# Macaron decoder layer on one core: order of the Strassen products, of the weight loads and of the norm statistics changed

## The chip, the core and the metric

The kernel runs on one core of a Trainium2 chip. The metric is device time in microseconds (us) of one execution of the whole layer; lower is better. TensorE is written PE, VectorE DVE, ScalarE ACT, GpSimd POOL, and SyncE SP, which issues most of the DMAs.

## The reference

One layer on x of 1024 tokens by 1024 features, float32, D_FF = 2816 (22 tiles of 128). The parts that the change touches are the two SwiGLU feed-forward networks (FFN) and the norms around them:

```python
h = rms_norm(x, ffn1_norm); x = x + 0.5 * (silu(h @ w_gate) * (h @ w_up)) @ w_down
h = rms_norm(x, mix_norm);  z = h @ w_in + b_in
...
x = x + merged @ w_out
h = rms_norm(x, ffn2_norm); x = x + 0.5 * (silu(h @ w_gate) * (h @ w_up)) @ w_down
return rms_norm(x, final_norm)
```

Between the FFNs stands a mixer: sliding-window attention and an mLSTM in parallel, gated and merged.

## The kernel before

All tensors lie with features on the 128 partitions and tokens along the free axis; the tokens are two halves of HS = 512, and x is KT = 8 feature tiles. TensorE multiplies with numbers split in two (`parted`, L325 to L328: ACT writes the high part, L327, VectorE the low part, L328), so every float32 product is three matmuls, high by high, high by low, low by high.

**Each FFN is done with seven products in place of eight** (a Strassen-Winograd scheme over the two halves of the tokens and two halves of the contracted features and of the columns). `PRODUCTS` (L29) gives the order of the products: 1, 2, 6, 7, 4, 5, 3. `gate_up` (L371) runs over 11 sets of a gate tile and an up tile, and in each set over the seven products, each in two groups w = 0 (gate) and 1 (up) of 12 matmuls at L413. `order` inside it lists (set, product): the first products 1 and 2 of the first LEAD = 4 sets come first, since they need only the first half of the tokens, then product 6 to 3 set by set. A weight block of 128x1024 is loaded by `load`, combined by `sum_of` (L403), and split one product ahead by `split`, into four rotating buffers `whi` and `wlo`. The products accumulate in PSUM banks `mm` (8, rotating); `product` (L404) lets product 2 write on into the bank of product 1 and product 3 into that of product 5:

```python
            key = {2: 1, 3: 5}.get(p, p)
            if first:
                st["ps", s, key, w] = psum.tile([128, HS], F32, name="mm")
```

so the first matmul of product 2 waits for ACT's copy of product 1 (L452), and that of product 3 for VectorE's sum with product 5 (L461). `gated` makes the SwiGLU (tanh on ACT, L421; two VectorE operations, L424 and L425). After a set, `paired` splits its results and stores them to `gd` in DRAM.

**The down part** (`ffn`) has 21 steps: three chunks (DOWN: 4, 4 and 3 column tiles) of seven products, each of 48 matmuls (L626; 36 in the last chunk). The moving operand of a step is fetched one step ahead from `gd` on POOL's queue (`fetch`, L564, 2 MB, two buffers); the weight blocks `dn` of a chunk, four of 1 MB (0.75 MB in the last), come on SP's queue (`load`, L555): for chunk 0 at the end of the last set's product 2, for chunk 1 at the end of its product 5, for chunk 2 at the step (1, 1). Results are added to x (L668, L669), and in the last chunk `done1` or `done2` adds up the squares of each finished x (`stats`: ACT square L252, VectorE add L254).

**The norms.** `rstd_of` (L256) sums the squares over the partitions by small matmuls (L261), adds epsilon (L263) and raises to -1/2 on POOL (L264); two turns later it spreads the result over the partitions by four transposes (L269, copy L271). `mixed` (L330) scales the second half of the tokens (L341) and makes the combined operands of products 6, 7, 4, 5, 3. `norm` (L282) scales the first half for the mixer: VectorE L297, ACT L298 for the high part, POOL L300 for the low part. These are generators: `lead` is advanced by `gate_up` between groups, those in `bg` by `pump`, one turn each; a `yield` is a turn, and so the number of turns sets where the work stands in each engine's queue. Engines run their instructions in program order.

**The order of the whole**: FFN 1, norm, mixer for the first 512 tokens, its residual at L1398, norm of the second half, mixer for the second half, its residual at L1469 (with `early` scaling the first half for FFN 2, L1437), FFN 2, final norm (`final`, L1497 and L1499).

## Time and profile before

| | |
|---|---|
| time, three executions | 2474.77, 2476.14 (median), 2485.99 us |
| the profiled execution | 2482.01 us, span 2479.4 us |
| TensorE busy | 2365.1 us, 95% |
| VectorE busy | 1740.1 us, 70% |
| ScalarE busy | 944.0 us, 38% |
| GpSimd busy | 258.0 us, 10% |
| mean granted TensorE clock | 0.976 of full |
| DMA | 361.44 MB, mean 146 GB/s |

The span is the time from the first to the last instruction in the profile. A busy time is a sum over an engine's instructions; the rows below place them. A timeline row gives start and duration (both in us), engine, line and operation, then tiles written and read, the count, and in brackets the idle time just before it and what ended that. The granted clock (PEclk) is 1.00 at the level of 2.4 GHz and 0.50 at 1.2 GHz.

### The profile page before, as it was taken

What the parts mean: (1) busy time and instruction counts of PE and PEld (TensorE: products, weight loads), DVE (VectorE), ACT (ScalarE), POOL (GpSimd) and SP (SyncE); (2) the same over time, 40 slices, a digit from 0 to 9 for tenths busy, and PEclk for the clock granted to TensorE, in tenths of its full rate; (3) what the DMA queues carried; (4) which work ended last, traced back from release to release, by engine and by line L of the source; (5) the groups of instructions that cost most, each with busy time, mean ns of one, the idle gap of its engine ahead of it and who ended that gap; (6) DMA issues with size and microseconds to landing.
All of it is one profiled execution on the core that took longest, in us unless ns stands there. A gap on an engine that the chain in (4) does not pass through costs nothing.

```text
span 2479.4 us, 30117 instructions
## 1 busy us (share of the span) xinstructions
PE 2365.1 (95%) x11094; PEld 1956.3 (79%) x11094; DVE 1740.1 (70%) x2780; ACT 944.0 (38%) x1664; POOL 258.0 (10%) x246
## 2 busy tenths in 40 slices
PE   7899999999998999999999999999899999999996
PEld 6788888778777878888877778888677888887885
DVE  6898888765768864554658944545589987886666
ACT  4333343312236642333346632333343443332223
POOL 0000000000044320000233400000000000000001
PEclk8999999999999999999999999999899999999997
DMA  4354453995631223222532122223524544569754
GB/s 172 100 197 163 153 165 132 339 319 187 208 126 52 73 62 92 75 81 84 173 109 64 52 79 87 79 79 99 186 98 162 191 148 146 171 231 331 250 176 138
DMA packets 154324, 361.44 MB, mean 146 GB/s; under 512 B 13505, under 2 KB 22849, under 8 KB 154177
## 3 DMA queue, kind: packets, MB, share of 16 engines
q1 hardware_dynamic: 131728, 277.79, 34.3%
q0 software_dynamic: 21584, 81.53, 9.6%
q8 instruction: 87, 1.43, 0.2%
q14 instruction: 61, 0.49, 0.1%
q10 hardware_dynamic: 864, 0.21, 0.0%
HBM read 263.27 MB, written 96.21 MB: 145 GB/s over the span
## 4 chain that ended last, share of the span: by engine, by line
PE 51%; DVE 12%; DMA 3%; ACT 3%; issue 3%; SPq 0%; DVEq 0%; POOL 0%; ACTq 0%; POOLq 0%
PE mm L413 14%; PE mm L308 7%; PE mm L310 7%; PE mm L309 7%; PE mm L626 5%; DMA gd<-nsq 2%; DVE P L1042 1%; PE mm L903 1%; DVE PT L1081 1%; PE mm L904 1%; PE mm L905 1%; DMA s<-gd 1%; DVE P L1062 1%; DVE wlo L87 1%; PE lm L1183 1%
## 5 line engine op out<-in xcount | busy, mean ns | idle before, releaser
L413 PE MATMUL mm<-s,whi 128*128 128x512 f32 x2112 | 659.6, 393 | 19.7 <-ACT nsq L452 9.4
L413 PEld LDWEIGHTS mm<-s,whi 128*128 128x128 f32 x2112 | 400.0, 190 | 107.1 <-ACT nsq L452 11.1
L308 PE MATMUL mm<-s,whi 128*128 128x512 f32 x1056 | 423.5, 401 | 0.9 <-DVE s L1368 0.9
L310 PE MATMUL mm<-s,wlo 128*128 128x512 f32 x1056 | 415.4, 393 | 1.5 <-POOL wlo L87 1.5
L309 PE MATMUL mm<-s,whi 128*128 128x512 f32 x1056 | 414.6, 393 | 0.0
L413 PE MATMUL mm<-s,wlo 128*128 128x512 f32 x1056 | 414.2, 392 | 0.0
L626 PE MATMUL mm<-s,whi 128*128 128x512 f32 (+1 forms) x1256 | 391.4, 394 | 15.3 <-DMA s<-gd 12.8
L626 PEld LDWEIGHTS mm<-s,whi 128*128 128x128 f32 x1256 | 239.8, 193 | 66.5 <-DMA s<-gd 6.3
L626 PE MATMUL mm<-s,wlo 128*128 128x512 f32 (+1 forms) x628 | 246.2, 392 | 0.0
L310 PEld LDWEIGHTS mm<-s,wlo 128*128 128x128 f32 x1056 | 199.9, 189 | 46.5 <-POOL wlo L87 3.2
L413 PEld LDWEIGHTS mm<-s,wlo 128*128 128x128 f32 x1056 | 200.4, 190 | 42.7 <-DVE wlo L328 0.8
L308 PEld LDWEIGHTS mm<-s,whi 128*128 128x128 f32 x1056 | 200.0, 189 | 42.4 <-issue 4.1
L309 PEld LDWEIGHTS mm<-s,whi 128*128 128x128 f32 x1056 | 200.3, 190 | 37.7
L87 DVE TENSOR_TENSOR wlo<-wraw,whi 128x1024 fp32r<-128x1024 f32 (+1 forms) x138 | 171.5, 1243 | 69.6 <-ACT whi L75 69.1
L75 ACT ACTIVATE whi<-wraw 128x1024 fp32r<-128x1024 f32 (+1 forms) x154 | 159.7, 1042 | 74.1 <-PE mm L310 23.7
L327 ACT ACTIVATE whi<-wr 128x1024 fp32r<-128x1024 f32 (+1 forms) x122 | 128.0, 1050 | 156.3 <-PE mm L413 92.8
L328 DVE TENSOR_TENSOR wlo<-wr,whi 128x1024 fp32r<-128x1024 f32 (+1 forms) x122 | 147.6, 1212 | 36.4 <-ACT whi L327 34.7
L327 ACT ACTIVATE whi<-s 128x1024 fp32r<-128x1024 f32 (+1 forms) x72 | 71.0, 986 | 238.2 <-PE mm L626 230.4
L564 POOL DMA_DIRECT2D s<-gd x42 | 31.8, 756 | 1188.5 <-DMA s<-dn 783.4
L626 PEld LDWEIGHTS mm<-s,wlo 128*128 128x128 f32 x628 | 121.1, 193 | 24.3
L328 DVE TENSOR_TENSOR nsq<-nsq 128x512 fp32r<-128x512 f32 x162 | 110.6, 686 | 31.6 <-ACT nsq L327 29.0
L413 PE MATMUL mm<-nsq,whi 128*128 128x512 f32 x352 | 113.3, 404 | 15.9 <-DVE nsq L461 15.9
(265 smaller groups left out, 3447.6 us busy)
## 6 DMA issues: line engine op xcount, KB each, us to landing
gd<-nsq SPq DMA_DIRECT2D x308, 256.0 KB, 3.0
s<-gd POOLq DMA_DIRECT2D x28, 2048.0 KB, 9.3
wraw<-win SPq DMA_DIRECT2D x84, 512.0 KB, 3.7
wr<-gu SPq DMA_DIRECT2D x74, 512.0 KB, 4.6
s<-gd POOLq DMA_DIRECT2D x14, 1536.0 KB, 6.9
s<-dn SPq DMA_DIRECT2D x16, 1024.0 KB, 11.2
wraw<-gu SPq DMA_DIRECT2D x30, 512.0 KB, 4.9
nsq<-x SPq DMA_DIRECT2D x32, 256.0 KB, 6.4
```

Source lines behind the costliest of these rows:

```text
L75: self.nc.scalar.activation(hv, v, AF.Copy)
L87: (self.nc.gpsimd if self.on_pool else self.nc.vector).tensor_sub(lv, v, hv.bitcast(F32))
L308: nc.tensor.matmul(ps, hi, xh, start=first, stop=False)
L309: nc.tensor.matmul(ps, hi, xl, start=False, stop=False)
L310: nc.tensor.matmul(ps, lo, xh, start=False, stop=last)
L327: nc.scalar.activation(hi, x, AF.Copy)
L328: nc.vector.tensor_sub(lo, x, hi.bitcast(F32))
L413: nc.tensor.matmul(ps, a[:, k], op[p](k, x), start=first and k == 0 and j == 0, stop=k == 3 and j == 2, skip_group_check=not first)
L564: nc.gpsimd.dma_start(t, gd[PRODUCTS.index(p), s0:s0 + a].rearrange("s p i t -> p s i t"))
L626: nc.tensor.matmul(ps, wt[:, f], t[:, f, x, c], start=first and f == 0 and q == 0, stop=f == a - 1 and q == 2, skip_group_check=not first)
L903: nc.tensor.matmul(ps, x[:, 0], hi, start=k == 0, stop=False)
L904: nc.tensor.matmul(ps, x[:, 1], hi, start=False, stop=False)
```

## The change

1. `rstd_of` is cut in two: `rstd_rows` (sums over the partitions) and `spread` (transposes and copy). The squares of the first half of FFN 2's norm are taken where that half is made, at the residual of the first mixer half (eight ACT squares, seven VectorE adds into `racc`, in `ev`), the sums in the second mixer half (`rows0`, a new constant `v0` holds the result), and `early` at the start of FFN 2 only spreads and scales.
2. In `gate_up` the first products are paired over sets: (0,1), (1,1), (0,2), (1,2), (2,1), (3,1), (2,2), (3,2) in place of (0,1), (0,2), (1,1), (1,2), and so on; the loads follow this order. `lead` of FFN 1 takes four turns before the second half's sums in place of two.
3. `PRODUCTS` ends 5, 4, 3 in place of 4, 5, 3, in `gate_up`, in the operands that `mixed` makes, and in the steps of the down part.
4. The `dn` blocks of chunks 1 and 2 are loaded one at a time, at the second to fifth step of the chunk before.
5. `norm` at the end of FFN 1 waits five turns in place of three, `final` at the end of FFN 2 five in place of two.

The diff, cut to its core (from L158 on the lines of the changed kernel are one higher, from about L290 eight higher, in the down part six, at the mixer's end six to twelve):

```diff
-PRODUCTS = (1, 2, 6, 7, 4, 5, 3)
+PRODUCTS = (1, 2, 6, 7, 5, 4, 3)
...
+    v0 = const("v0", [128, 4])
...
-    def rstd_of(pool, psum, acc, n=4):
+    def rstd_rows(psum, acc, v, n=4):
...
-        v = pool.tile([128, 4], F32, name="nv", bufs=1)[:, :n]
         nc.vector.tensor_scalar(v, ps[:, :, 0], EPS, None, op0=OP.add)
         nc.gpsimd.tensor_tensor(v, v, mhalf[:, :n], op=OP.pow)
-        yield
-        yield
+
+    def spread(pool, psum, v, n=4):
+
         ps = psum.tile([128, 128 * n], F32, name="mm")
...
-        yield r
+        return r
+
+    def rstd_of(pool, psum, acc, n=4):
+        v = pool.tile([128, 4], F32, name="nv", bufs=1)[:, :n]
+        rstd_rows(psum, acc, v, n)
+        yield
+        yield
+        yield spread(pool, psum, v, n)
...
-        for p, m, h in ((4, 4, 0), (5, 0, 1)):
+        for p, m, h in ((5, 0, 1), (4, 4, 0)):
...
-                key, to, m, half = {4: (7, 1, 1, 0), 5: (7, 7, 1, 1), 3: (6, 6, 0, 1)}[p]
+                key, to, m, half = {5: (7, 1, 1, 1), 4: (7, 7, 1, 0), 3: (6, 6, 0, 1)}[p]
...
-        order = [(s, p) for s in range(LEAD) for p in (1, 2)]
+        order = [(s, p) for s0 in range(0, LEAD, 2) for p in (1, 2) for s in (s0, s0 + 1)]
         for s in range(S2):
-            for p in (6, 7, 4, 5, 3):
+            for p in PRODUCTS[2:]:
...
-        def load(c, i):
+        def load(c, b):
...
+            if b == 0:
+                raw[c] = slot((0, 2, 0)[c], [16 * HS], F32)
+            m, h = divmod(b, 2)
...
             if p == 2:
-                load(0, 0)
+                for b in range(4):
+                    load(0, b)
...
-            elif p == 5:
-                load(1, 2)
...
-            if (c, p) == (1, 1):
-                load(2, 0)
+            if 1 <= i % 7 <= 4 and c < last:
+                load(c + 1, i % 7 - 1)
...
         def lead():
-            yield
-            yield
+            for _ in range(4):
+                yield
...
-                    bg.append(norm(pool, psum, lambda k: X[k][0], 1, Hm[0], acc=Hm[1]))
+                    bg.append(norm(pool, psum, lambda k: X[k][0], 1, Hm[0], acc=Hm[1], wait=5))
...
                 nc.sync.dma_start(xd[0, :, d], xr[d])
+                sq = racc if d == 0 else op.tile([128, HS], F32, name="rsq", bufs=1)
+                nc.scalar.activation(sq, xr[d], AF.Square)
+                if d:
+                    nc.vector.tensor_add(racc, racc, sq)
...
+    def rows0():
+        for _ in range(6):
+            yield
+        rstd_rows(psum, [racc], v0)
+
+    bg.append(rows0())
...
     def early():
         yield
-        for k in range(KT):
-            stats(pool, acc[0], X[k][0], k == 0)
-            yield
+        r = spread(pool, psum, v0)
         yield
-        for r in rstd_of(pool, psum, acc[:1]):
-            yield
...
-        for _ in range(0 if p == end else 2):
+        for _ in range(0 if p == end else 5):
```

**Places where instructions move.** The first is ScalarE in sets 0 to 3 of FFN 1. L452 (after: L460) copies product 1 out of its bank; L327 (L335) is the high part of a weight block, L421 (L429) the tanh, L271 (L272) the copy of the spread norm, L345 and L348 (L353, L356) are `mixed`'s casts, which wait for VectorE. Before:

```order
L271 ACTIVATE nsq_354<-mm_349 128x512
L327 ACTIVATE whi_386<-wr_213 128x1024
L452 ACTIVATE nsq_392<-mm_373 128x512
L345 ACTIVATE s1_135<-nsq_394 128x512
L348 ACTIVATE s1_135<-nsq_137 128x512
L452 ACTIVATE nsq_415<-mm_402 128x512
L345 ACTIVATE s1_135<-nsq_417 128x512
L348 ACTIVATE s1_135<-nsq_139 128x512
```

After:

```order
L460 ACTIVATE nsq_364<-mm_351 128x512
L335 ACTIVATE whi_378<-wraw_282 128x1024
L429 ACTIVATE nsq_382<-mm_294 128x512
L272 ACTIVATE nsq_389<-mm_384 128x512
L353 ACTIVATE s1_136<-nsq_408 128x512
L356 ACTIVATE s1_136<-nsq_138 128x512
L335 ACTIVATE whi_426<-wr_214 128x1024
L429 ACTIVATE nsq_432<-mm_324 128x512
L353 ACTIVATE s1_136<-nsq_436 128x512
L356 ACTIVATE s1_136<-nsq_140 128x512
L335 ACTIVATE whi_473<-wraw_284 128x1024
L460 ACTIVATE nsq_484<-mm_460 128x512
```

Before, a copy of product 1 stood directly ahead of the casts of one turn; now the four copies of sets 0 and 1 come first, ahead of all casts, and the copy of set 2 (nsq_484) stands behind two turns of them.

The second is VectorE at the end of the second mixer half, ahead of FFN 2. L1469 (L1481) is the residual of one feature tile, L254 (L255) adds squares (before: into nsq_13623 for the first half, nsq_13624 for the second), L1437 (L1449) scales a tile of the first half, L328 (L336) is its low part, L87 the low part of a mixer weight. Before:

```order
L1469 SCALAR_TENSOR_TENSOR nsq_13641<-mm_13647,nsq_13641 128x512
L254 TENSOR_TENSOR nsq_13623<-nsq_13623,nsq_13682 128x512
L254 TENSOR_TENSOR nsq_13623<-nsq_13623,nsq_13699 128x512
L87 TENSOR_TENSOR wlo_13705<-wraw_13596,whi_13685 128x1024
L254 TENSOR_TENSOR nsq_13623<-nsq_13623,nsq_13715 128x512
L1469 SCALAR_TENSOR_TENSOR nsq_13645<-mm_13689,nsq_13645 128x512
L254 TENSOR_TENSOR nsq_13624<-nsq_13624,nsq_13726 128x512
L254 TENSOR_TENSOR nsq_13623<-nsq_13623,nsq_13729 128x512
L254 TENSOR_TENSOR nsq_13623<-nsq_13623,nsq_13746 128x512
L87 TENSOR_TENSOR wlo_13752<-wraw_13662,whi_13732 128x1024
L254 TENSOR_TENSOR nsq_13623<-nsq_13623,nsq_13762 128x512
L1469 SCALAR_TENSOR_TENSOR nsq_13687<-mm_13736,nsq_13687 128x512
```

After:

```order
L1481 SCALAR_TENSOR_TENSOR nsq_13671<-mm_13677,nsq_13671 128x512
L1449 SCALAR_TENSOR_TENSOR nsq_13655<-nsq_13655,gains_68,nsq_13705 128x512
L336 TENSOR_TENSOR s0_13653<-nsq_13655,s0_13653 128x512
L1449 SCALAR_TENSOR_TENSOR nsq_13657<-nsq_13657,gains_68,nsq_13705 128x512
L336 TENSOR_TENSOR s0_13653<-nsq_13657,s0_13653 128x512
L87 TENSOR_TENSOR wlo_13740<-wraw_13627,whi_13720 128x1024
L1449 SCALAR_TENSOR_TENSOR nsq_13659<-nsq_13659,gains_68,nsq_13705 128x512
L336 TENSOR_TENSOR s0_13653<-nsq_13659,s0_13653 128x512
L1481 SCALAR_TENSOR_TENSOR nsq_13675<-mm_13724,nsq_13675 128x512
L255 TENSOR_TENSOR nsq_13654<-nsq_13654,nsq_13761 128x512
L1449 SCALAR_TENSOR_TENSOR nsq_13661<-nsq_13661,gains_68,nsq_13705 128x512
L336 TENSOR_TENSOR s0_13653<-nsq_13661,s0_13653 128x512
```

The adds for the first half are gone, and the scaling begins behind the first residual, where before it began behind the fourth (row 1828, after L263).

The third is VectorE at the end of FFN 1's down part. L668 and L669 (L674, L675) add to x, L263 is the norm's epsilon, L297 (L305) a scaling of `norm`, L87 the low part of a mixer weight. Before:

```order
L263 TENSOR_SCALAR nv_5058<-mm_5053 128x4
L668 TENSOR_TENSOR nsq_4033<-nsq_4033,nsq_4752 128x512
L669 TENSOR_TENSOR nsq_4033<-mm_5061,nsq_4033 128x512
L87 TENSOR_TENSOR wlo_5093<-wraw_4720,whi_5091 128x816
L668 TENSOR_TENSOR nsq_4035<-nsq_4035,nsq_4768 128x512
L669 TENSOR_TENSOR nsq_4035<-mm_5081,nsq_4035 128x512
L297 SCALAR_TENSOR_TENSOR nsq_5100<-nsq_3697,gains_68,nsq_5079 128x512
L297 SCALAR_TENSOR_TENSOR nsq_5103<-nsq_3954,gains_68,nsq_5079 128x512
L668 TENSOR_TENSOR nsq_4037<-nsq_4037,nsq_4781 128x512
L669 TENSOR_TENSOR nsq_4037<-mm_5107,nsq_4037 128x512
L297 SCALAR_TENSOR_TENSOR nsq_5120<-nsq_3699,gains_68,nsq_5079 128x512
L297 SCALAR_TENSOR_TENSOR nsq_5124<-nsq_3956,gains_68,nsq_5079 128x512
```

After:

```order
L255 TENSOR_TENSOR nsq_4801<-nsq_4801,nsq_5096 128x512
L87 TENSOR_TENSOR wlo_5110<-wraw_4723,whi_5108 128x816
L675 TENSOR_TENSOR nsq_3866<-mm_4964,nsq_3866 128x512
L675 TENSOR_TENSOR nsq_3868<-mm_4981,nsq_3868 128x512
L263 TENSOR_SCALAR nv_5127<-mm_5128 128x4
L675 TENSOR_TENSOR nsq_3870<-mm_4994,nsq_3870 128x512
L675 TENSOR_TENSOR nsq_3872<-mm_5011,nsq_3872 128x512
L305 SCALAR_TENSOR_TENSOR nsq_5164<-nsq_3693,gains_68,nsq_5151 128x512
L305 SCALAR_TENSOR_TENSOR nsq_5167<-nsq_3953,gains_68,nsq_5151 128x512
L305 SCALAR_TENSOR_TENSOR nsq_5171<-nsq_3695,gains_68,nsq_5151 128x512
L305 SCALAR_TENSOR_TENSOR nsq_5175<-nsq_3955,gains_68,nsq_5151 128x512
L305 SCALAR_TENSOR_TENSOR nsq_5179<-nsq_3697,gains_68,nsq_5151 128x512
```

The adds of squares (L255) now stand in the last step but one (before, in the last but two), the scalings stand in one piece behind the last four additions to x; before, they alternated with the additions of the last two products.

## Rows read from the trace of the kernel before

**Rows 1.** The page: busy us of each engine, share of the span, instructions

```profile
PE 2365.1 (95%) x11094; PEld 1956.3 (79%) x11094; DVE 1740.1 (70%) x2780; ACT 944.0 (38%) x1664; POOL 258.0 (10%) x246
```

**Rows 2.** TensorE's waits by line and releaser: us in total, times, longest us

```profile
PE mm L261 <- DVE nsq L254: 21.5, 7, 5.3
...
PE mm L413 <- DVE nsq L461: 15.9, 6, 5.4
...
PE mm L626 <- DMA s<-gd: 12.8, 6, 3.3
...
PE mm L413 <- ACT nsq L452: 9.4, 4, 4.0
```

**Rows 3.** Windows: busy us of PE, PEld, DVE, ACT, POOL (counts); clock; DMA share, GB/s

```profile
33.20:39.90 6.70, 6.70 (x21) 5.49 (x21) 3.76 (x5) 2.67 (x4) 1.01 (x1) 0.51 0.49 157
...
63.90:67.20 3.30, 3.30 (x9) 2.56 (x9) 3.27 (x5) 0.08 (x1) 0.00 (x0) 0.52 0.48 116
...
108.30:115.00 6.70, 5.21 (x13) 4.17 (x14) 6.10 (x12) 1.58 (x2) 0.00 (x0) 0.51 0.31 92
```

**Rows 4.** TensorE's timeline, FFN 1's first sets

```profile
32.94 1.84 PE L261 MATMUL mm<-mean,nsq 128*128 128x2 f32 x8 [3.02 <-DVE nsq L254]
...
63.54 1.14 PE L413 MATMUL mm<-s,whi 128*128 128x512 f32 x2 [4.03 <-ACT nsq L452]
...
109.79 1.19 PE L413 MATMUL mm<-nsq,whi 128*128 128x512 f32 x2 [5.36 <-DVE nsq L461]
```

**Rows 5.** Busy us by stretch, first sets and a stretch without a stall

```profile
43.80:78.40 34.60, 30.57 (x128) 24.84 (x127) 29.18 (x42) 14.30 (x23) 0.00 (x0) 0.95 0.21 62
...
78.40:103.20 24.80, 24.19 (x107) 19.69 (x107) 24.28 (x40) 9.78 (x15) 0.35 (x1) 1.00 0.39 114
...
350.00:400.00 50.00, 50.00 (x222) 41.40 (x222) 41.85 (x55) 19.85 (x27) 0.00 (x0) 1.00 0.46 152
```

**Rows 6.** TensorE's timeline, ahead of FFN 2

```profile
1756.13 0.37 PE L261 MATMUL mm<-mean,nsq 128*128 128x2 f32 x1 [4.96 <-DVE nsq L254]
...
1790.12 0.80 PE L413 MATMUL mm<-s,whi 128*128 128x512 f32 x1 [5.74 <-ACT whi L327]
```

**Rows 7.** VectorE's timeline, ahead of FFN 2

```profile
1741.96 0.69 DVE L1469 SCALAR_TENSOR_TENSOR nsq<-mm,nsq 128x512 f32<-128x512 f32 x1 [8.05 <-DMA nsq<-xd]
...
1751.67 1.22 DVE L87 TENSOR_TENSOR wlo<-wraw,whi 128x1024 fp32r<-128x1024 f32 x1
...
1777.45 0.68 DVE L1469 SCALAR_TENSOR_TENSOR nsq<-mm,nsq 128x512 f32<-128x512 f32 x1
...
1779.51 0.74 DVE L1437 SCALAR_TENSOR_TENSOR nsq<-nsq,gains 128x512 f32<-128x512 f32 x1
...
1781.56 0.75 DVE L1437 SCALAR_TENSOR_TENSOR nsq<-nsq,gains 128x512 f32<-128x512 f32 x1
```

**Rows 8.** Busy us, clock, DMA share, GB/s, first chunk of FFN 1's down part

```profile
455.00:520.00 65.00, 59.70 (x248) 48.46 (x247) 47.66 (x60) 19.64 (x27) 2.23 (x3) 0.95 1.08 393
```

**Rows 9.** TensorE's timeline, first step of the second chunk

```profile
558.23 0.47 PE L626 MATMUL mm<-s,whi 128*128 128x512 f32 x1 [3.03 <-DMA s<-gd]
```

**Rows 10.** DMA issues, 430 to 580: count, KB each, median us to landing

```profile
s<-gd POOLq DMA_DIRECT2D x10, 2048.0 KB, 11.9
```

**Rows 11.** Timelines of TensorE, VectorE and GpSimd, end of FFN 1

```profile
682.81 0.37 PE L261 MATMUL mm<-mean,nsq 128*128 128x2 f32 x1 [3.72 <-DVE nsq L254]
...
692.85 1.41 DVE L297 SCALAR_TENSOR_TENSOR nsq<-nsq,gains 128x512 f32<-128x512 f32 x2
...
703.97 3.07 DVE L297 SCALAR_TENSOR_TENSOR nsq<-nsq,gains 128x512 f32<-128x512 f32 x2
...
694.34 6.31 POOL L300 TENSOR_TENSOR s<-nsq,s 128x512 fp32r<-128x512 f32 x4 [7.64 <-ACT s L298]
```

**Rows 12.** TensorE's timeline, norm between the mixer halves

```profile
1211.69 1.05 PE L261 MATMUL mm<-mean,nacc 128*128 128x2 f32 x8 [1.08 <-DVE nacc L254]
```

**Rows 13.** VectorE's timeline, end of FFN 2

```profile
2442.03 0.69 DVE L669 TENSOR_TENSOR nsq<-mm,nsq 128x512 f32<-128x512 f32 x1 [2.94 <-PE mm L626]
```

More of the change, by code (lines that the diff above doesn't have):

```diff
@@ L280, in rstd_task, with norm @@
             yield
-    def norm(pool, psum, xs, which, H, acc=None, eng=nc.vector):
+    def norm(pool, psum, xs, which, H, acc=None, eng=nc.vector, wait=3):
         if acc is None:
@@ L288, in norm @@
                 yield
-        for _ in range(3):
+        for _ in range(wait):
             yield
@@ L496, in gate_up @@
             split(*next(rest))
-        for h in range(2):
-            load(3, 0, h)
-        early.clear()
         yield
@@ L510, in prepare @@
             done += 1
-            if done == 4:
+            if done == 3:
+                load(3, 0, 0), load(3, 0, 1)
+                early.clear()
+            elif done == 4:
                 load(0, 1, 0), load(0, 1, 1)
-            elif done == 6:
+            elif done == 7:
                 load(0, 0, 1)
@@ L1445, in lead2 @@
         yield
-        for r in rstd_of(pool, psum, acc[1:]):
+        for r in rstd_of(pool, psum, [acc]):
             yield
@@ L1470, in layer @@
         nc.sync.dma_start(xd[1, :, d], x)
[L1471 removed]
+        stats(pool, acc, x, d == 0)
         pump()
```

27 lines of the change are left out of this document (11 added, 16 removed).

## The prediction

> **What bounds the kernel now.** I read the views in this order: busy shares, waits of TensorE, stretches by granted clock, single stalls in TensorE's timeline, then the timelines of the engines it waits for. TensorE is busy 95% of a span of 2479.4 us, VectorE 70% [rows 1], so time can only come out of TensorE's gaps and its slow stretches; the matmuls themselves stay, but for eight small ones that move from one place to another. The view of TensorE's waits [rows 2] holds the gaps that this change is near: 21.5 us at L261 (the small matmuls that sum a norm's squares, waiting for VectorE's adds L254), 15.9 us at L413 for VectorE's L461, 12.8 us at L626 for a fetched block, 9.4 us at L413 for ScalarE's copy L452.
>
> A gap costs more than its length. After the stall of 3.02 us at 32.94 [rows 4] the granted clock is 0.51 (the 1.2 GHz level) for 6.7 us, all of it filled with matmuls; after 109.79 it is 0.51 with 5.21 us of matmuls [rows 3]. At the full level [rows 5] the same matmuls take half: so a long gap costs another 3.4 or 2.6 us. After the stall at 63.54 the slow stretch is 3.3 us, clock 0.52 [rows 3]: half of it, 1.7, is what I charge for such a short one, and for new gaps as well.
>
> A full-speed matmul is 50.00/222 = 0.225 us [rows 5], a half product of 24 is 5.4 us, a step of 48 is 10.8 us.
>
> **First FFN, start (pairing of first products, earlier norm).** Product 2 writes on into the bank of product 1, so it waits for the copy L452. Before, (1,2) followed (1,1) directly: 4.03 us lost at 63.54 [rows 4]. Paired, the other set's product stands between, a whole product (5.4 us per half) of slack. The norm of the second half starts one product later, so that L254's adds are done: 3.02 gone at 32.94. The last stall, 5.36 at 109.79, is product 3 waiting for L461 of product 5, whose bank it continues; in the new order product 4 stands between. Removed: 3.0 + 3.4, 4.0 + 1.7, 0.6 (rest of the 9.4 here) and 5.4 + 2.6 = 20.7 us.
> But VectorE can't follow so far. It is busy 29.18 of 34.6 us and then 24.28 of 24.8 [rows 5]: 5.9 us of idle in all. My walk starts its run about 3.6 earlier. So it can come to L461 of set 0 at most 9.5 earlier, 100.3, and about 3 earlier again because product 5's work now precedes product 4's: 97.4. TensorE would be there at 94.8. So 2.6 us of wait remain, and 1.7 of slow clock. On ScalarE the copies of the first products of sets 2 and 3 now stand behind casts that wait for VectorE (front matter, first order listing): I estimate 1.5 and 1.4. New: 7.2. **Net -13.5**; ends -20.7 (no new wait) and -5 (VectorE gains nothing but half its idle).
>
> **Product 3 elsewhere.** L413 waiting for L461 is 15.9 in 6 places; 5.4 is booked above and 3.3 comes below. The other four sum to 7.2, and one of them has a slow stretch of 1.6. One product of slack is 5.4 us, longer than any of them. **-8.8**, ends -8.8 and -5.
>
> **Second FFN, start (squares taken earlier).** Eight squares and seven adds leave the queues ahead of the scaling of the first half (second order listing). The stall of 4.96 at 1756.13 goes, and so could the 5.74 at 1790.12 [rows 6]. What is late next is VectorE: its first row there is the residual at 1741.96, after an idle time for a DMA [rows 7]. From its end, 1742.6, it still has eight scalings with their subtractions at 2.05 (1779.51 to 1781.56), eight residual-and-add pairs at 2.1 (1777.45 to 1779.51) and seven weight splits at 1.22 [rows 7]: 16.4 + 16.8 + 8.5 = 41.7, so the first product starts near 1784.3, not 1790.1. That is -5.8, and -2 for a slow stretch less: **-7.8**. Inside, TensorE will stall twice for the splits, about 4 us each, in place of the two old stalls. Ends: 0, if VectorE doesn't start earlier than its DMA; -11, if only TensorE's own work counts (5.7 and 5.0 both go).
>
> **Second FFN, first products.** The same pairing takes the other half of the 9.4 (4.8), the 3.3 at product 3 and two short slow stretches (3.4): 11.5. As in the first FFN two or three waits come back; no norm work fills VectorE's queue as full, so I take 4.4. **-7**, ends -11.5 and -3.
>
> **Down blocks, one a step.** Of three bursts of four block loads in each FFN, two are now spread over steps 1 to 4 and 8 to 11. After such a burst the fetches ran late; the wait at 558.23, 3.03 us, was the worst of the first FFN [rows 9]. All waits for a fetch are 12.8 in 6 places [rows 2]; three of them are long enough for a slow stretch, by the prices above 5.9 together: 18.7 at stake. Spread, a step carries a fetch of 2.10 MB, a block of 1.05 MB and, in three steps of the first chunk, x rows of 1.05 MB: 4.20 MB. The chip moved 393 GB/s in the dense stretch [rows 8], 4.24 MB in a step of 10.8 us. So in chunk 0 the steps are just full: I let 5.8 us of waits stand there, where 5.5 stood, and take away 558.23 with its slow stretch (4.6) and, in the second FFN, 0.8 and a slow stretch of 2.8. **-7.5**, ends -18.7 and +6 (eight carrying steps of chunk 0 wait 0.8 more each).
> The fetch lands 11.9 us after its issue [rows 10], longer than a step: there is no room in it. The Trainium skill, "DMA: Bandwidth & Descriptors", section "Queues, rings and completion order", says that each of the 16 DMA engines goes round the queues it has work for, a packet at a time; a block beside every fetch would then slow each fetch, and the sum would lose the 7.5 and more. This speaks against the change and is the third rival below; no row here shows a fetch beside exactly one block.
>
> **End of the first FFN.** With product 4 a step later the squares of the first half end in the last step but one, and the norm waits 5 turns, into the last step. The stall of 3.72 at 682.81 [rows 11] stays in part, 2.5. All eight scalings (third order listing) and so all eight GpSimd subtractions now come after the last step. GpSimd needs 6.31 for four [rows 11], 1.6 each; four of them lay beside the last step. The mixer's first matmuls consume these rows in order and hide half of the 6.3: +3.3, and 1.2 of slow clock. **+4.5**, ends 0 and +8. VectorE's scalings are slower beside GpSimd, too: two took 1.41 alone and 3.07 beside it [rows 11]; eight in a row are 5.6 to 12.3. The Trainium skill, "GPSIMD Engine Reference", section "1. Specifications", says GpSimd's SBUF interfaces are shared with VectorE; the trace agrees by these two rows, and with a share for all eight the term would be at its upper end.
>
> **Between the mixer halves.** The squares of the first half go to ScalarE (38% busy) and seven adds of 0.69 to VectorE, which idles there for DMAs. They stand ahead of the adds that L261 waits for at 1211.69, 1.08 now [rows 12]; I add 1.5. Eight small matmuls take 1.05 there [rows 12], and the moved ones as much: +1.0. **+2.5**, ends +1 and +5.
>
> **End of the second FFN.** The norm of the first half comes a step later. VectorE ends the kernel and has one hole, 2.94 us at 2442.03 [rows 13], which the later work can fill. **-2**, ends -5 and +3.
>
> **Sum.** -13.5 - 8.8 - 7.8 - 7 - 7.5 + 4.5 + 2.5 - 2 = -39.6. The profiled execution took 2482.0; that gives 2442.4. It is 5.9 over the median of the other three, 2476.14; the middle of all four is 2479.1, from which the sum gives 2439.5. I say **2440**. The likeliest case's own range, part of the ends, is 2426 to 2453.
>
> **Rivals.**
> (1) VectorE sets the pace in sets 0 to 3 of both FFNs, and a gap closed at one place opens at the next. For: 24.28 of 24.8 us busy. Against: 5.4 us idle in the stretch before. Then the pairing gives 5 and 3 instead of 13.5 and 7: 2440 + 12.5 = 2452.
> (2) The pairing does not do what it says: the copies on ScalarE, queued behind the casts, come so late that product 2 waits as before (9.4 and 3.4 slow stay). For: the order listing. Against: ScalarE is 38% busy. 2440 + 10 (the rest of the new waits replaced) = 2450.
> (3) Slower, by the fetches. If each block beside a fetch takes a share of the engines as in the sentence on the skill, then all 16 steps that carry a block (four in each of the first two chunks, two FFNs) wait. Each 1 us of wait is 16 us. Without any gain of the loads the sum is 2447; to be slower by 0.5%, 2488.5, it takes 41.5/16 = 2.6 us a step: a median landing near 13.5 us in place of 11.9. For: no room now. Against: 3.15 MB in steps without x rows is far below 4.24, and a burst of four blocks cost 3.03 once, so one costs nearer 0.8. A mild form, 0.8 in each of the 16, is +12.8 on 2447: 2460.
>
> **Chances.** Forecast 0.58, (1) 0.18, (2) 0.10, (3) mild 0.10, (3) full 0.04. The range 2424 to 2462 holds all but the full third rival and the tails of the others. Half a per cent is 12.4 us, about what a measurement of this kernel can tell; the bounds are 2463.8 and 2488.5. Faster 0.86 (the first four cases, less their tails), same 0.10, slower 0.04.
>
> **What would show it.** Right: no wait for the copy of product 1 in set 1 and none for L469 (old L461) after set 0; a wait near 2.6 for product 3 of set 0; the second FFN's first product near 5.8 us earlier than the savings before it alone give; no wait over 2 us for a fetch in step 7; GpSimd's eight subtractions in one piece after the last step, with TensorE waiting some 3 us in the first mixer blocks. Wrong: fetch landings over 13 us, waits for L469 in many sets, or a clock that is no fuller for fewer gaps.

## The result, and the profile after

The changed kernel took 2460.82 us (median of 6 runs, 2460.06 to 2461.28), the kernel before 2480.97 (6 runs, 2474.77 to 2490.23): a ratio of 0.9916, 95% interval 0.9895 to 0.9938. It is faster by about 20 us, 0.8%. The forecast was 2440, from 2424 to 2462: the sign is right, the time lies at the upper end of the range, and the gain is half of the 39.6 of the sum. The profiled execution took 2461.28 us with a span of 2459.5, 19.9 less than before.

The page of the changed kernel, busy time of each engine (before: [rows 1]):

```profile
PE 2357.0 (96%) x11094; PEld 1951.4 (79%) x11094; DVE 1741.3 (71%) x2780; ACT 940.8 (38%) x1664; POOL 259.6 (11%) x246
```

TensorE has the same 11094 matmuls and is busy 8.1 us less: so much of the gain is slow clock that went. The rest is waits. TensorE's waits in the changed kernel (line, releaser, us in total, times, longest):

```profile
PE mm L632 <- DMA s<-gd: 12.8, 6, 3.4
PE mm L262 <- DVE nsq L255: 9.1, 2, 7.7
...
PE mm L421 <- ACT nsq L460: 8.7, 2, 4.7
PE mm L270 <- POOL nv L264: 8.6, 3, 5.1
...
PE mm L262 <- DVE nacc L255: 4.6, 1, 4.6
PE mm L421 <- DVE nsq L469: 4.3, 4, 2.3
```

Against [rows 2]: the waits for the adds of squares fell from 21.5 to 9.1, those of product 3 from 15.9 to 4.3; those for fetched blocks are 12.8 as before, those for the copy of product 1 8.7 in place of 9.4; those for nacc, between the mixer halves, grew from 1.1 to 4.6, and those for GpSimd's small power (L264) from 3.5 to 8.6.

Both kernels run the same matmuls, so the n-th matmul of a stage can be looked up in both timelines. The difference of its start, after less before, shows where the time goes:

| stage (up to the start of) | forecast | before to after |
|---|---|---|
| start of FFN 1 (product after (0,3): 117.75, now 108.31) | -13.5 | -9.4 |
| product 3 elsewhere, both FFNs | -8.8 | -7.7 |
| down part of FFN 1 (first step 472.89, now 458.10; ninth 570.80, now 557.80) | -7.5 with the next | +1.8 |
| down part of FFN 2 (first step 2227.60, now 2209.29; ninth 2324.07, now 2302.67) | | -3.1 |
| end of FFN 1 (first matmul of the mixer at L308, after: L316, 717.46, now 707.76) | +4.5 | +3.3 |
| between the mixer halves, to the end of the second half | +2.5 | +7.4 |
| start of FFN 2 (its second product 1798.65, now 1787.45) | -7.8 | -8.9 |
| first products of FFN 2 | -7 | -4.8 |
| end of FFN 2 | -2 | +1.5 |
| sum | -39.6 | -19.9 |

Three views of the changed kernel show the terms that fell short. First TensorE's timeline at the start of FFN 1 and in the first chunk of its down part (start, duration, line, tiles, idle time before and its releaser):

```profile
67.05 0.73 PE L421 MATMUL mm<-s,whi 128*128 128x512 f32 x2 [4.05 <-ACT nsq L460]
...
101.17 0.70 PE L421 MATMUL mm<-nsq,whi 128*128 128x512 f32 x2 [2.30 <-DVE nsq L469]
...
482.44 0.73 PE L632 MATMUL mm<-s,whi 128*128 128x512 f32 x2 [2.42 <-DMA s<-gd]
...
507.87 0.74 PE L632 MATMUL mm<-s,whi 128*128 128x512 f32 x2 [3.35 <-DMA s<-gd]
...
545.22 0.70 PE L632 MATMUL mm<-s,whi 128*128 128x512 f32 x2 [2.81 <-DMA s<-gd]
```

The wait for the copy of product 1 is still there and as long as in [rows 4]. Counted by matmuls it is at (2,2), and so was the one before: the wait at 63.54 is the first group of (2,2), not (1,2) as the prediction has it. Product 3 of set 0 waits 2.30; I had said 2.6. And the down part waits for its fetches as before, also at step 7 (545.22), where I had taken the wait of [rows 9] away.

Second, VectorE, ScalarE and TensorE between the mixer halves, in the changed kernel's timeline. L1405 is the residual, L1408 and L1410 the new square and add for the first half, L253 and L255 square and add for the second half (nacc):

```profile
1203.05 0.68 DVE L1405 SCALAR_TENSOR_TENSOR xr<-mm,xr 128x512 f32<-128x512 f32 x1
1204.43 0.69 DVE L1410 TENSOR_TENSOR zb<-zb,rsq 128x512 f32<-128x512 f32 x1 [0.70 <-ACT rsq L1408]
1205.04 0.68 DVE L255 TENSOR_TENSOR nacc<-nacc,nsq 128x512 f32<-128x512 f32 x1
...
1203.77 0.63 ACT L1408 ACTIVATE rsq<-xr 128x512 f32<-128x512 f32 x1 [2.50 <-DVE xr L1405]
1204.30 0.61 ACT L253 ACTIVATE nsq<-m 128x512 f32<-128x512 f32 x1
...
1205.78 1.86 PE L262 MATMUL mm<-mean,nacc 128*128 128x2 f32 x8 [4.56 <-DVE nacc L255]
```

ScalarE stood still for 2.50 us ahead of L1408, which waits for a residual on VectorE, and the last square of the second half (L253) is behind it in its queue. VectorE's add then waits for ScalarE's square, and TensorE for that add: 4.56 in place of 1.08 [rows 12].

Third, the ends. GpSimd and VectorE at the end of FFN 1, and TensorE's stall near the end of FFN 2:

```profile
687.47 13.09 POOL L308 TENSOR_TENSOR s<-nsq,s 128x512 fp32r<-128x512 f32 x8 [5.96 <-ACT s L306]
...
685.99 10.48 DVE L305 SCALAR_TENSOR_TENSOR nsq<-nsq,gains 128x512 f32<-128x512 f32 x8
...
2427.30 1.86 PE L262 MATMUL mm<-mean,nsq 128*128 128x2 f32 x8 [7.75 <-DVE nsq L255]
```

All eight subtractions now lie in one piece behind the last step, as forecast, and the eight scalings take 10.48 us beside them.

### The profile page after: what moved, and what is told of

It is laid out like the page before. It is cut to its first block, busy times and chain, and to the rows that moved or that the text cites. A ratio compares the mean times of both kernels' runs of the same rounds, so it can differ in the third digit from the quotient of the medians.

```text
span 2459.5 us, 30117 instructions
## 1 busy us (share of the span) xinstructions
PE 2357.0 (96%) x11094; PEld 1951.4 (79%) x11094; DVE 1741.3 (71%) x2780; ACT 940.8 (38%) x1664; POOL 259.6 (11%) x246
## 3 DMA queue, kind: packets, MB, share of 16 engines
q1 hardware_dynamic: 131728, 277.79, 34.5%
## 4 chain that ended last, share of the span: by engine, by line
PE 58%; DVE 16%; issue 16%; DMA 5%; ACT 3%; POOL 1%; SPq 0%; DVEq 0%; POOLq 0%; ACTq 0%
PE mm L421 15%; PE mm L632 11%; PE mm L316 8%; PE mm L318 7%; PE mm L317 7%; DMA s<-gd 3%; DVE P L1048 1%; PE mm L909 1%; DVE PT L1087 1%; PE mm L910 1%; PE mm L911 1%; DMA gd<-nsq 1%; DVE wlo L336 1%; DVE P L1068 1%; DVE wlo L87 1%
## 5 line engine op out<-in xcount | busy, mean ns | idle before, releaser
L421 PE MATMUL mm<-s,whi 128*128 128x512 f32 x2112 | 657.4, 392 | 13.5 <-ACT nsq L460 8.7
L421 PEld LDWEIGHTS mm<-s,whi 128*128 128x128 f32 x2112 | 399.3, 189 | 99.9 <-ACT nsq L460 9.5
L316 PE MATMUL mm<-s,whi 128*128 128x512 f32 x1056 | 424.4, 402 | 1.0 <-ACT whi L75 1.0
L421 PE MATMUL mm<-s,wlo 128*128 128x512 f32 x1056 | 413.7, 392 | 0.0
L632 PE MATMUL mm<-s,whi 128*128 128x512 f32 (+1 forms) x1256 | 388.2, 391 | 14.0 <-DMA s<-gd 12.8
L632 PEld LDWEIGHTS mm<-s,whi 128*128 128x128 f32 x1256 | 237.7, 192 | 65.0 <-issue 10.3
L316 PEld LDWEIGHTS mm<-s,whi 128*128 128x128 f32 x1056 | 200.7, 190 | 42.7 <-issue 2.8
L421 PEld LDWEIGHTS mm<-s,wlo 128*128 128x128 f32 x1056 | 200.0, 189 | 41.6
L87 DVE TENSOR_TENSOR wlo<-wraw,whi 128x1024 fp32r<-128x1024 f32 (+1 forms) x138 | 169.6, 1229 | 67.2 <-ACT whi L75 66.6
L335 ACT ACTIVATE whi<-wr 128x1024 fp32r<-128x1024 f32 (+1 forms) x122 | 127.8, 1048 | 129.7 <-PE mm L421 83.3
L336 DVE TENSOR_TENSOR wlo<-wr,whi 128x1024 fp32r<-128x1024 f32 (+1 forms) x122 | 147.8, 1212 | 36.6 <-ACT whi L335 36.6
L335 ACT ACTIVATE whi<-s 128x1024 fp32r<-128x1024 f32 (+1 forms) x72 | 71.1, 987 | 250.9 <-PE mm L632 239.0
L336 DVE TENSOR_TENSOR nsq<-nsq 128x512 fp32r<-128x512 f32 x162 | 110.4, 685 | 24.4 <-ACT nsq L335 23.9
L429 ACT ACTIVATE nsq<-nsq 128x512 f32<-128x512 f32 x66 | 41.8, 633 | 216.6 <-DVE nsq L469 205.2
```

Of the source, the lines that this page charges most:

```text
L87: (self.nc.gpsimd if self.on_pool else self.nc.vector).tensor_sub(lv, v, hv.bitcast(F32))
L316: nc.tensor.matmul(ps, hi, xh, start=first, stop=False)
L335: nc.scalar.activation(hi, x, AF.Copy)
L336: nc.vector.tensor_sub(lo, x, hi.bitcast(F32))
L421: nc.tensor.matmul(ps, a[:, k], op[p](k, x), start=first and k == 0 and j == 0, stop=k == 3 and j == 2, skip_group_check=not first)
L429: nc.scalar.activation(t, z[0], AF.Tanh, scale=0.5)
```

## The experiments

Where a result is "profile +x", it is the same comparison of matmul starts as in the table, against the changed kernel's profiled execution. All kernels were timed beside the kernel before, whose medians were 2480.6, 2483.2 and 2481.2 in the three sittings.

**Order of the products undone** (L29, with the tables that belong to it):

```diff
-PRODUCTS = (1, 2, 6, 7, 5, 4, 3)
+PRODUCTS = (1, 2, 6, 7, 4, 5, 3)
...
-        for p, m, h in ((5, 0, 1), (4, 4, 0)):
+        for p, m, h in ((4, 4, 0), (5, 0, 1)):
```

> The changed kernel with the old order of the products, 4, 5, 3. Theory (each part does what the two traces, set side by side, show): the waits of product 3 for the sum with product 5 come back: 3.1 and 1.7 of slow clock at the last set of the first FFN, 0.4 at the third, 0.8 and 1.6 in the second FFN, and about 5 at set 0 of either FFN; 12 to 16 us over the changed kernel, 2473 to 2477 us. Rival (VectorE sets the pace of the first sets, a gap closed there only opens another): the waits at set 0 stay as they are and only the later ones come back, 7 us, about 2468.

2469.7 us (7 runs), ratio 0.9956 (0.9939 to 0.9973). Its timeline at set 0:

```profile
106.01 1.19 PE L421 MATMUL mm<-nsq,whi 128*128 128x512 f32 x2 [8.21 <-DVE nsq L469]
```

Profile: +6.7 at set 0 of FFN 1, +4.0 at its last set, +5.8 at set 0 of FFN 2: the new order is the largest part of what the gate and up parts gain. But -5.8 came back in the first eight steps of the down part, -3.2 at the end of FFN 1 and -1.3 at the end of FFN 2. So the theory's waits all returned, and still the total is 9, not 12 to 16: the new order pays back in the down part. At the ends of the two FFNs that is product 4, which it makes late there; why the first eight steps differ is left open below.

**Pairing undone**:

```diff
-        order = [(s, p) for s0 in range(0, LEAD, 2) for p in (1, 2) for s in (s0, s0 + 1)]
+        order = [(s, p) for s in range(LEAD) for p in (1, 2)]
...
-            for _ in range(4):
+            for _ in range(2):
```

> The changed kernel with the old order of the first products, (0,1), (0,2), (1,1), (1,2), its loads and the two turns ahead of the norm. Theory: the gain of the pairing is the 4.0 at the first norm with its slow stretch of 3.4, the wait for the copy of product 1 mostly moved, not gone (4.05 at 67.05 in place of 4.03 at 63.54); undone costs 4 to 8 us in the first FFN and 0 to 2 in the second, 2465 to 2470. Rival (the pairing is worth what was forecast): 13 or more, 2474.

2461.86 us (4 runs), ratio 0.9922 (0.9900 to 0.9944): no different from the changed kernel. Two rows of its timeline:

```profile
62.73 1.22 PE L421 MATMUL mm<-s,whi 128*128 128x512 f32 x2 [4.03 <-ACT nsq L460]
...
103.17 0.70 PE L421 MATMUL mm<-nsq,whi 128*128 128x512 f32 x2 [0.74 <-DVE self L208]
```

It is 3.6 us behind at the first product 6, which follows the first products, and 0.4 behind after (0,3): what the pairing gains is lost again at set 0, where product 3 of the paired kernel waits 2.30 and this one 0.74. With the new order of the products the pairing is worth nothing that can be measured. In the sum it had 12.7 us in the first FFN (3.0 + 3.4, 4.0 + 1.7, 0.6), less 2.9 of new waits; even the theory allowed it more than it has.

**Block loads undone** (`load` issues four blocks again, at `tail(5)` and at step (1,1)):

```diff
-            if 1 <= i % 7 <= 4 and c < last:
-                load(c + 1, i % 7 - 1)
+            if (c, p) == (1, 1):
+                load(2, 0)
...
+            elif p == 5:
+                load(1, 2)
```

> The changed kernel with the old bursts of four block loads. Theory (the loads are not paced by the steps: SP issues them as soon as their buffer is free, so chunk 2's blocks still meet the fetch for step 7): within 3 us of the changed kernel, 2459 to 2464; the first FFN's down part 1 to 2 us shorter, the second's about 3 longer. Rival (blocks one a step relieve the fetches, as forecast): 7.5 slower, 2468.

2465.96 us (10 runs, 2458.96 to 2476.33), ratio 0.9941 (0.9925 to 0.9956), some 5 us slower by the medians, with intervals that overlap. Profile: -0.3 in the down part of FFN 1 up to step 4 and +0.1 to step 8, so the new loads are worth nothing there; +4.8 in FFN 2's first four steps. The 4.8 is not clear of chance: the next kernel has +3.6 at the same place with its loads unchanged. Neither theory is borne out as a whole: the loads do nothing in the first FFN, as the theory had it, and something up to 5 us in the second.

**Early squares undone** (no squares in `ev`, no `rows0`; `early` takes them as before; 35 lines of difference):

```diff
-                sq = racc if d == 0 else op.tile([128, HS], F32, name="rsq", bufs=1)
-                nc.scalar.activation(sq, xr[d], AF.Square)
-                if d:
-                    nc.vector.tensor_add(racc, racc, sq)
...
+        for k in range(KT):
+            stats(pool, acc[0], X[k][0], k == 0)
+            yield
```

> The changed kernel with the squares of the second FFN's first half taken again at the start of that FFN. Theory: about 9 us come back there, but the norm between the mixer halves gets back the 3.5 of its wait, some 1.1 of slow clock and the small sums, 7 us in all: 1 to 3 us over the changed kernel, 2462 to 2464, with the wait of L262 for nacc near 1.1 again. Rival (the norm between the halves is late for another reason): the wait of 4.6 stays, 2468 to 2470.

2466.93 us (6 runs), ratio 0.9945 (0.9927 to 0.9963). The wait between the halves (waits of TensorE, 1190 to 1215):

```profile
PE mm L262 <- DVE nacc L255: 1.2, 1, 1.2
```

Profile: -4.5 there, -2.1 more in the second half, +8.6 at the start of FFN 2. That is the theory, +2 in sum; the median is 6 over, with 3.6 of it at FFN 2's first fetches, which this edit doesn't touch.

**The waits of the norms undone** (wait 3 and 2 in place of 5 and 5):

```diff
-                    bg.append(norm(pool, psum, lambda k: X[k][0], 1, Hm[0], acc=Hm[1], wait=5))
+                    bg.append(norm(pool, psum, lambda k: X[k][0], 1, Hm[0], acc=Hm[1], wait=3))
...
-        for _ in range(0 if p == end else 5):
+        for _ in range(0 if p == end else 2):
```

> The changed kernel with the old waits of the norms at the ends of the two FFNs (3 and 2 turns). Theory (the later norm at the end of the first FFN comes from the order of the products, not from the wait; at the end of the second FFN the small sums stand too early in either case): TensorE's start of the mixer within 1 us of the changed kernel, the stall at L262 near the end grows from 7.8 to 9 or more; in all 0 to 3 us slower, 2461 to 2464. Rival (the longer waits push the scalings behind the last step and cost the 3.3 us): 3 us faster, 2458.

2462.67 us (4 runs), ratio 0.9920 (0.9891 to 0.9949). Profile: +2.4 at the end of FFN 1, 0.0 at the end of FFN 2. The longer wait is a gain of some 2 us there (kernels with the same waits differ there by up to 1) and no loss: the 3.3 of that term belong to the order.

**Norm between the halves later; last norm later**:

```diff
-        bg.append(norm(op, psum, lambda k: xb[:, k], 1, Hcur))
+        bg.append(norm(op, psum, lambda k: xb[:, k], 1, Hcur, wait=6))
...
-        for _ in range(0 if p == end else 5):
+        for _ in range(0 if p == end else 9):
```

> The changed kernel with the norm between the mixer halves waiting 6 turns in place of 3 and the last norm of the first half 9 in place of 5: two places far apart, read each by its own stretch. Theory (the wait of 4.6 at L262 for nacc is a turn set too early: the last square of the second half stands on ScalarE behind a square of the first half that waits for the residual): the wait falls under 1.2 us and its slow stretch goes, 4 to 5 us come back by the first matmul of the second mixer half. At the end the stall of 7.8 falls to about 4 and 0 to 3 us come back. In all 2453 to 2457. Rival (the norm is then late for the mixer): the first blocks of the second mixer half wait 3 us and more for GpSimd, nothing gained.

2459.55 us (4 runs: 2453.88, 2456.18, 2462.92, 2464.99), ratio 0.9909 (0.9876 to 0.9942). Profile: no wait for nacc any more and -4.0 at that place, as the theory had it, though TensorE now waits 2.2 for GpSimd's small power behind it; -0.7 at the end of FFN 2. But the profiled execution is one of the two long ones: 15 us in the mixer ran at the low clock, 5.6 us lost at a place that the edit doesn't touch (windows; columns as in [rows 3]):

```profile
1275.00:1290.00 15.00, 12.18 (x60) 9.13 (x60) 10.91 (x40) 8.35 (x18) 7.16 (x3) 0.96 0.32 108
1290.00:1305.00 15.00, 15.00 (x56) 11.28 (x55) 5.71 (x23) 6.35 (x19) 3.51 (x2) 0.50 0.13 36
```

So the median says nothing here, the place does.

**Blocks on GpSimd's queue**:

```diff
-            nc.sync.dma_start(t.rearrange("p (d x) -> p d x", d=4),
+            (nc.gpsimd if c else nc.sync).dma_start(t.rearrange("p (d x) -> p d x", d=4),
```

> The changed kernel with the blocks of chunks 1 and 2 issued on GpSimd's queue, each behind the fetch of its step, so that they are paced by the steps. Theory (the first chunk's steps are bound by the DMA, and blocks of chunk 2 that run ahead on SP take 3.1 MB out of it): the wait at step 7 goes, and one of the two others; 4 to 8 us less in the first FFN's down part, 2 to 4 in the second's, 2449 to 2455. Rival (a block in the same queue delays the next fetch): waits for a fetch in most steps that carry a block, slower than 2465.

2454.89 us (4 runs, 2448.72 to 2454.96), ratio 0.9884 (0.9855 to 0.9913). The fetch for step 7, in the changed kernel (issued at 531.84) and in this one (528.60; count, KB, us to landing):

```profile
s<-gd POOLq DMA_DIRECT2D x1, 2048.0 KB, 13.3
```

```profile
s<-gd POOLq DMA_DIRECT2D x1, 2048.0 KB, 8.3
```

It lands in 8.3 us in place of 13.3, less than a step, and the wait at step 7 is gone. So it is in every trace: this fetch took 13.0 to 13.5 us in all eleven with the blocks on SP's queue (the kernel before and two of the changed one among them), 8.0 to 8.3 in the three with the blocks of chunks 1 and 2 on GpSimd's. The fetches for steps 2 to 5, which have a block of chunk 1 beside them in both, take 12.5 to 13.8 in the changed kernel and 10.3 to 14.4 here; waits of 0.9 and 2.8 remain at steps 3 and 4. The two windows from 430 to 570, changed kernel first, move the same bytes:

```profile
430.00:570.00 140.00, 131.41 (x563) 107.51 (x562) 94.88 (x118) 37.37 (x47) 8.39 (x11) 0.98 0.89 318
```

```profile
430.00:570.00 140.00, 136.31 (x593) 112.00 (x592) 99.76 (x121) 38.30 (x48) 12.92 (x17) 0.99 0.90 318
```

Both at 318 GB/s, but TensorE does 30 matmuls more. Profile: -2.1 up to step 4, another -4.7 up to step 8 of FFN 1. In FFN 2 +0.6 (+2.9 and -2.2), where the theory expected 2 to 4 less. Why the blocks were in the way is seen on SP's queue in the changed kernel:

```profile
497.85 0.38 SPq L562 DMA_DIRECT2D s<-dn  x1
...
505.19 23.10 SPq L562 DMA_DIRECT2D s<-dn  x5
...
523.14 5.15 SPq L562 DMA_DIRECT2D s<-dn  x4
```

"One a step" is an order in the program only. The blocks of chunk 2 were meant for steps 8 to 11, from 558 on; SP has no work that ties it to a step, so it went on to them at 505, right behind chunk 1's last block, was held by their buffer until 523, issued them by 528 (the row of five merges chunk 1's last block with them, the last row has chunk 2's four alone), and they met the fetch for step 7. On GpSimd's queue each stands behind a fetch that waits for TensorE, and so keeps its step.

**Late x loads swapped; four subtractions on GpSimd**:

```diff
-                    loadx(d, i - 3)
+                    loadx(d, 4 - i)
...
-            nc.vector.tensor_sub(X[4 + k][0], X[4 + k][0], X[k][0])
+            nc.gpsimd.tensor_sub(X[4 + k][0], X[4 + k][0], X[k][0])
```

> The changed kernel with two edits in places far apart, read each by its own stretch: the two late loads of x in the down part in the order in which the new order of the products needs them, and the four subtractions that prepare product 4's difference in each FFN on GpSimd in place of VectorE (2.8 us of VectorE's work). Theory (VectorE sets the pace in sets 0 to 2): the wait of product 3 in set 0 falls from 2.3 to under 1 and set 1 begins 1 to 3 us earlier in the first FFN; the wait of VectorE for x, 7.8 us, goes, with at most 1 us for TensorE. 2457 to 2460. Rival (GpSimd slows VectorE by as much as it takes over): no change at set 0.

2460.15 us (4 runs, 2454.52 to 2465.26), ratio 0.9904 (0.9868 to 0.9940). At set 0 nothing moved (0.0, wait 2.23). VectorE's operations ahead of L344, in the changed kernel and in this one (40 to 102 us; count, busy us, mean ns):

```profile
L342 DVE TENSOR_TENSOR s<-nsq,s 128x512 fp32r<-128x512 f32 x4 | 2.7, 685 | 0.0
L343 DVE TENSOR_TENSOR s<-nsq,s 128x512 fp32r<-128x512 f32 x4 | 2.7, 685 | 0.0
```

```profile
L342 DVE TENSOR_TENSOR s<-nsq,s 128x512 fp32r<-128x512 f32 x4 | 3.8, 960 | 0.0
L343 DVE TENSOR_TENSOR s<-nsq,s 128x512 fp32r<-128x512 f32 x4 | 3.8, 952 | 0.0
```

The eight operations beside GpSimd grew by 2.2 us, 2.7 had been taken away: the rival. The wait for x (7.8 us on VectorE) went, without a gain for TensorE.

**The mixer's constants later** (a test of VectorE without GpSimd):

```diff
-            bg.append(late_consts(pool))
+            def later():
+                for _ in range(40):
+                    yield
+                yield from late_consts(pool)
+            bg.append(later())
```

> The changed kernel with the small constants of the mixer made 40 turns later, so that their VectorE operations (nine, about 2 us) no longer stand ahead of L469 at set 0 of the first FFN. Theory (VectorE sets the pace there): the wait of product 3 at set 0 falls from 2.3 to under 0.8 and the next product starts 1.5 to 2.3 us earlier; up to the whole of it may be lost again at the first chunk of the down part, which the DMA bounds, so 2458 to 2461 in all. Rival (the wait comes from ScalarE or the weights): the wait stays at 2.3.

2458.51 us (4 runs, 2452.42 to 2460.79), ratio 0.9909 (0.9892 to 0.9925). Profile: -2.3 from the first product 6 to the product after (0,3), kept to the end of the gate and up part. The wait itself:

```profile
99.61 0.70 PE L421 MATMUL mm<-nsq,whi 128*128 128x512 f32 x2 [1.59 <-DVE nsq L469]
```

The time is what the theory said, the wait is not: it shrank by 0.7, not below 0.8, and the other 1.6 of the 2.3 is the slow stretch that followed the wait of 2.30 and doesn't follow one of 1.59. That VectorE's work is what TensorE waits for there is borne out by this, and VectorE is busy 31.49 of the 32 us from 70 to 102 in the changed kernel. The edit moves a little else too: five small DMA issues on ScalarE's queue (86.42 to 89.66), ahead of a weight split, and one operation of 0.35 us on GpSimd; their share was not tested apart.

**Four edits together, and with the down part in the old order.** The first takes over the blocks on GpSimd's queue, the norm between the halves at 6 turns, the last norm at 9, the constants later. The second keeps all but the 9, and adds:

```diff
-        steps = [(c, p) for c in range(len(DOWN)) for p in PRODUCTS]
+        steps = [(c, p) for c in range(len(DOWN)) for p in (1, 2, 6, 7, 4, 5, 3)]
```

> The changed kernel with four edits together: blocks of chunks 1 and 2 on GpSimd's queue, the norm between the halves 6 turns late, the last norm 9, the constants 40 turns later. If the pieces add up: 6.3 + 4.0 + 0.7 + 1 less than the changed kernel, 2449, between 2445 and 2452. If gains of different places are swallowed by the next bound: 2453 to 2456.

> As the kernel before in this list, but the last norm at 5 turns again, and the steps of the down part in the old order 4, 5, 3, while the first part of the FFN keeps 5, 4, 3. Theory (the later product 4 in the down part is what costs 3.3 us at the end of the first FFN and 1.3 at the end of the second; the gain of the new order lies in the first part alone): 3 to 5 us less than that kernel, 2441 to 2449. Rival (the loss at the end of the first FFN comes from the 5 turns): the same as that kernel.

> The changed kernel again, beside the others on their chip: 2460 to 2465 by what its parts showed; a spread of more than 5 us between executions, as the kernels with one part changed had, would make differences under 3 us between them no finding.

| kernel | us, median of 4 runs | lowest to highest | ratio to before |
|---|---|---|---|
| four edits | 2449.08 | 2443.72 to 2453.66 | 0.9875 (0.9854 to 0.9897) |
| the same, down part 4, 5, 3 | 2446.69 | 2443.41 to 2448.27 | 0.9863 (0.9848 to 0.9878) |
| the changed kernel again | 2458.61 | 2455.79 to 2463.30 | 0.9915 (0.9900 to 0.9930) |

The pieces add up: in both, profile -2.3 at set 0 and -4.7 to -4.9 between steps 4 and 8 of FFN 1's down part; -3.6 and -2.2 between the halves; and with the old order in the down part -3.4 at the end of FFN 1 and -1.3 at the end of FFN 2, about what undoing the whole order gave back there (-3.2 and -1.3). The last norm at 9 turns gave nothing here (0.0; alone it was -0.7). The kernel with the old order in the down part has the lowest median: 12 us under the changed kernel on the same chip, 34.5 under the kernel before. Between it and the one with four edits the intervals overlap, and the changed kernel, at 2458.61 below what was expected of it, spread by 7.5 us, so by what was set down beforehand a difference of medians under 3 us is no finding; the two places, measured twice each, are what speaks for it.

## Why the prediction was right, and why it was half too much

**Right.** The direction, and four of eight terms within 2.5 us, one of them by luck. Product 3 elsewhere (-7.7 for -8.8): one product of slack was enough but for 1.34 of 1.72 us at (2,3), and undoing the order brought the waits back. The end of FFN 1 (+3.3 for +4.5): the eight subtractions behind the last step; that the stall at 682.81 shrinks was said there but not booked, and it shrank to 1.33. The first products of FFN 2 (-4.8 for -7): the new wait there was 4.66, all of it at (3,2), for the 4.4 that I took, and 1.7 of slow clock came with it.

**Right by luck: the start of FFN 2** (-8.9 for -7.8). The time fits, 1781.2 against a forecast 1784.3, less the 2.3 us by which everything ahead stood earlier, 1782.0. But the forecast has VectorE's remaining work set the start, and counts eight residual-and-add pairs in it; in the trace six stand there (the first residual needs no add, the last comes behind the start), and VectorE idles. TensorE's stalls for weight splits, VectorE's idle time, and a window up to the first product (columns as in [rows 3]):

```profile
1754.32 0.80 PE L318 MATMUL mm<-s,wlo 128*128 128x512 f32 x1 [2.23 <-DVE wlo L87]
...
1763.60 0.50 PE L318 MATMUL mm<-s,wlo 128*128 128x512 f32 x1 [1.98 <-DVE wlo L87]
...
1775.96 0.69 DVE L1481 SCALAR_TENSOR_TENSOR nsq<-mm,nsq 128x512 f32<-128x512 f32 x1 [3.36 <-PE mm L318]
```

```profile
1763.60:1781.20 17.60, 17.60 (x70) 14.41 (x71) 10.11 (x12) 6.32 (x8) 0.00 (x0) 0.90 0.74 237
```

TensorE is busy all of the last 17.6 us, and VectorE waits for it. So TensorE's own work set the start, behind stalls of 1.0, 2.2 and 2.0 us; the two for the splits were forecast, at twice the size.

**The first step that failed: "take away 558.23 with its slow stretch".** It rested on the words that a step carries one block. The program's order was read as a time. SP's queue issued them as soon as their buffer allowed it, from 523 on, some 35 us ahead of their first step; the wait at step 7 stayed (2.81 for 3.03), and the down part of FFN 1 became 1.8 us longer, where I had a gain of 4.3. (The 1.8 itself isn't clear of chance: the changed kernel's second trace is 2.5 shorter there.) Moving the blocks to a queue that is paced took the wait at step 7 away in three kernels of three, -4.7 to -4.9 between steps 4 and 8, where the changed kernel's second trace has -1.5, and shows that the size of the term was fair and its cause misread. Beside chunk 2's four blocks the fetch took 13.3 us, without them 8.3. The Trainium skill, "DMA: Bandwidth & Descriptors", section "Issuing engines are not separate DMA queues", says that DMAs from different engines run on the same 16 DMA engines and interleave; the two landings agree with that. A slip of the sum besides: the parts given there, 4.6 + 0.8 + 2.8 less 0.3, make 7.9, not 7.5.

**The second: "VectorE, which idles there for DMAs"** (between the halves, +7.4 for +2.5). The adds were hidden, as I said. What was not counted is ScalarE's queue: I moved eight squares to it by its busy share (38%), though each of them waits for a residual, and whatever stands behind it waits with it. That is 3.5 us of wait and 1.4 of slow clock. The small matmuls are the +1.0 that I had (0.9), and a slow stretch at 1331 that costs 1.6 comes on top. Two runs show the mechanism: without the squares the wait is 1.2, with the norm three turns later it is nil and 4.0 us come back (2.2 of wait for the small power are new there).

**The third: the two places of the pairing** (-9.4 for -13.5 and -4.8 for -7). The step "Before, (1,2) followed (1,1) directly: 4.03 us lost at 63.54" has the place and the cause wrong. The wait was at (2,2), and no product 2 of set 1 waited in either kernel; the copy of (2,1) was late because it stands on ScalarE behind a cast that waits for VectorE, in both. ScalarE before, then VectorE and ScalarE after:

```profile
59.98 0.63 ACT L345 ACTIVATE s<-nsq 128x512 fp32r<-128x512 f32 x1 [5.93 <-DVE nsq L344]
...
62.91 1.06 ACT L452 ACTIVATE nsq<-mm 128x512 f32<-128x512 f32 x2
```

```profile
59.85 1.23 DVE L411 TENSOR_TENSOR wraw<-wraw,wr 128x1024 f32<-128x1024 f32 x1 [1.86 <-DMA wraw<-gu]
...
64.43 0.63 ACT L353 ACTIVATE s<-nsq 128x512 fp32r<-128x512 f32 x1 [7.47 <-DVE nsq L352]
...
66.42 0.58 ACT L460 ACTIVATE nsq<-mm 128x512 f32<-128x512 f32 x1
```

A product of slack didn't remove that: where the sum had new waits of 1.5 and 1.4, there were 4.05 in one piece with 1.9 of slow clock after it. VectorE waits 1.9 us for a weight block, and has its sums to do, ahead of the value for ScalarE's cast. This is rival 2 in its mechanism, the copy behind the casts, and rival 1, a gap that opens at the next place, in part; undoing the pairing alone cost nothing. The earlier norm gave 4.3 of its 6.4. The wait at set 0 came out as worked out, 2.30 for 2.6, but both its ends stood some 4 us later than worked out (TensorE was there at 98.87 for 94.8). What gained at the start of FFN 1 is the order of the products.

**The fourth: "the later work can fill" the hole at the end of FFN 2** (+1.5 for -2). The squares of the half that is scaled there end a step later, TensorE waits 7.75 us for them in place of 3.72, and behind that its waits are 7.0 us in place of 9.7 (the longest 5.1, for GpSimd's small power at 2442.62), so that only 2.6 of the 4.0 come back. With the old order in the down part the kernel gets 1.3 back, twice.

Of the rivals, the DMA one (mild, 2460) gives the measured time almost exactly, but by another way than it says: there was no 0.8 us in each step, and three of the four shortfalls have nothing to do with these fetches. On GpSimd the prediction was right to weigh the shared interfaces: ten instead of five and a half us for eight scalings beside it, and 685 to 960 ns for VectorE's subtractions in the experiment. The Trainium skill, "GPSIMD Engine Reference", section "1. Specifications", names the sharing; these runs agree.

**Left open.** How much the block loads are worth in FFN 2: its first four steps differ by up to 4 us between kernels that issue the same DMAs there. And why 5.8 us came back in the down part when the order was undone: 4.0 us of gap stand ahead of it at the last set, which the DMAs may use to get ahead (not tested), and the rest lies within what these steps differ by between kernels with the same loads, -2.8 to +1.1.

## What to carry to other kernels

Work that is put on an engine in program order isn't put at a time: a DMA queue with nothing that waits for the step runs ahead of it, and an instruction that waits holds all behind it, however idle its engine is by the page. So for each moved instruction look for what it waits for and what stands behind it, and to pace a transfer, queue it behind something that is paced. When an order helps one stage and hurts the next, give each stage its own.
